# Loads of W of the in-projection issued by PoolE from the second quad on

## The chip, the core and the metric

The kernel runs on one core of one Trainium2 chip. The metric is the device time of one execution in microseconds (us); three executions of the kernel before are given. One further execution was taken by the hardware profiler, and all rows quoted below come from it. "Span" is the time from the program's first instruction to its last in that execution.

Engines are named as the profile names them: PE (TensorE matmul), PEld (its weight loads), DVE (VectorE), ACT (ScalarE), POOL (GpSimd, "PoolE" in the title) and SP (SyncE). SP does no arithmetic here; it only issues DMAs. SPq and POOLq in a row stand for the sequencer of that engine, which waits and issues.

## The reference

A decoder block with two mixing branches, cut to what matters here:

```
proj = x @ w_in[l] + b_in[l]          # x (2048, 1024), w_in (1024, 9216)
q, k, v, g_attn, u_lru, g_lru, gate_logits = split(proj)
attn  = three groups of causal dilated attention over rope(q), rope(k), v
y_a   = (attn * silu(g_attn)) @ w_attn_proj
h     = rg_lru(causal_conv(u_lru))
y_b   = (h * silu(g_lru)) @ w_lru_proj
merged = sigmoid(gA) * y_a + sigmoid(gB) * y_b
x     = layer_norm(alpha * x + merged @ w_out + b_out)
```

All is float32. The first line, the in-projection, is the largest part, and the change touches it alone.

## The kernel before

The program has three stages one after the other: the in-projection (with rope, the convolution, the recurrence and the gates folded in) up to about 1442 us of the span, the attention up to about 1640 us, and the output part.

**Quads.** The in-projection is cut into 72 quads, `s` = 0 to 71. A quad computes two tiles of 128 output columns for two chunks of 512 positions; quads 0 to 35 go over all 72 column tiles with the first two chunks, quads 36 to 71 over the same tiles with the last two. Over the 1024 inputs a quad is a 2 by 2 block product, done in seven block products in the manner of Strassen and Winograd instead of eight (quads 0 and 36 are plain, eight). One block product is a *job*: 12 matmuls of 128x128 by 128x512, four slices of the inputs by three terms (high by high, high by low, low by high part of a float32 value).

**What a quad needs of W.** Four blocks of W, A11, A12, A21 and A22, 128 partitions by 512 elements (256 KB) each, and four sums of them: S1 = A21 + A22, S2 = S1 + A11, S3 = A21 + A11, S4 = S2 + A12. ACT copies each of the seven into a high part `h`, DVE subtracts to get the low part `l` (`prep_w`), and PE multiplies with both. In the first 36 quads S1 and S3 start as two loads of A21, into which POOL adds A22 and A11 by an accumulating DMA (`added`, line 245); the low parts are stored to `wl_scr`. In the last 36 quads DVE forms the sums, POOL forms S4, and the low parts are loaded back from `wl_scr` (`load_lo`, line 287).

**Order.** Nothing is scheduled by a tool: the code walks over the jobs T, and each engine's instructions stand in the order in which this walk emits them. Each engine works through its own list strictly in order, and an instruction that waits for a semaphore holds all that stand behind it on that engine. `at(t, fn)` puts a piece of work at a job. With t0 three or four jobs ahead of a quad's first job, a quad of the first half loads S1 and S3 six jobs ahead of t0, A11 four, A12 three, A22 mostly a job before t0 or later, and adds into S1 and S3 four jobs ahead; DVE's first sum stands one job ahead of t0. In the second half A21 and A22 are loaded four jobs and A11 and A12 three jobs ahead of t0.

**Slots.** All these tiles, and also x, q, k, v and the recurrence's temporaries, live in 34 slots of 256 KB that are handed out in the order in which they were given back (`take`, `give`). A load has to wait until the slot's last reader, an engine or a store, is done.

**Who issues.** Before the change SP issues almost all DMAs: the loads of W (line 234), of x (221), the partition swaps for rope (`sw`, 307), the stores of low parts (282), of q, k and v (330, 337, 347, 371), of the recurrence's input (`u_scr`, 377) and others. POOL issues the accumulating DMAs, 64 small loads for the recurrence's gates (441) and four of a bias (445, 446), and does some arithmetic, mostly in the second half of the quads (S4, half of rope, the gating of the recurrence's output).

**The start.** The code first emits, on SP: A11 of quad 0, four blocks of x, A12, four blocks of x, A21 and A22, then eight blocks of x; only then come the five loads of quad 1. PE begins when the first W block and the first x block are there and split.

Of the kernel before, what the change touches and what calls it, by code (L numbers as in the profile page):

```python
# [15 lines left out]
P = 128  # L16
S = 2048
# [14 lines left out]
def hybrid_block_kernel(ctx: ExitStack, tc: tile.TileContext, a: dict, out: bass.AP):  # L32
    nc = tc.nc
    sp, act, dve, pool, pe = nc.sync, nc.scalar, nc.vector, nc.gpsimd, nc.tensor
# [98 lines left out]
    def take(name, dt=F32R):  # L133
        if not vacant:
            raise RuntimeError(f"no slot at {now['n']}: {[x[1].name if hasattr(x[1],'name') else x[1] for x in home.values()]} chains {len(chains)}")
        i = vacant[0]
        if name[0] == "y" and now["n"] >= base[NQ - 1]:
            i = next((x for x in LATE if x in vacant), i)
            if i in LATE:
                LATE.remove(i)  # L140
        vacant.remove(i)
        t = sl_p.tile([P, CH], dt, tag=f"s{i}", name=name)
        home[id(t)] = (i, t)
        return t
# [86 lines left out]

    def load_w(s, n):
        r = raw[s, n] = take(f"w{n}_{s}", F32)
        sp.dma_start(r.rearrange("p (k f) -> p k f", f=P), w_part(s, "A21" if n[0] == "S" else n))

    def w_part(s, n):

        f = plan[s][1][int(n[1]) - 1][0]
        k = 4 * (int(n[2]) - 1)
        return a["w_in"][f, :, k:k + 4, :]  # L240
# [461 lines left out]
    for s in range(1, NQ):  # L702
        t0 = base[s] - (3 if plan[s][0] else 4)
        if plan[s][2] is None:
            for d, n in ((4, "A21"), (4, "A11"), (3, "A22"), (3, "A12")):
                at(t0 - d, lambda s=s, n=n: load_w(s, n))
            for j in range(4):
                at(t0 + j, lambda s=s, j=j: prep_w(s, j))
            continue
        if plan[s][0]:  # L710
            for d, n in ((4, "A21"), (4, "A22"), (3, "A11"), (3, "A12")):
                at(t0 - d, lambda s=s, n=n: load_w(s, n))
        else:
            d22 = 3 if s == 1 else 4 - plan[s][2].index(4)
            for d, n in ((6, "S1"), (6, "S3"), (4, "A11"), (3, "A12"), (d22, "A22")):
                at(t0 - d, lambda s=s, n=n: load_w(s, n))
            for n, x in (("S1", "A22"), ("S3", "A11")):
                at(max(t0 - 4, 2), lambda s=s, n=n, x=x: added(s, n, x))
        at(max(t0 - 1, 4), lambda s=s: sums(s))
        at(max(t0, 4), lambda s=s: add_w(s, "S4", "S2", "A12"))  # L720
        if plan[s][0]:
            at(t0, lambda s=s: sum3(s))
        for j in range(7):
            d = 3 if j == 6 and plan[s][2] is MID else 0
            if plan[s][0] and j % 2 == 0:
                at(t0 + j - 1 + d, lambda s=s, j=j: load_lo(s, j))
            at(t0 + j + d, lambda s=s, j=j: prep_w(s, j))
# [244 lines left out]
    n = len(where)  # L972
# [416 lines left out]
    for n in range(32):  # L1389
        c, f = divmod(n, 8)  # L1390
# [229 lines left out]
```

## Time and profile before

| what | us |
|---|---|
| median of three executions | 2099.08 |
| lowest and highest of them | 2097.64 and 2104.75 |
| the profiled execution, own time | 2101.99 |
| its span | 2100.3 |
| SP's loads of W (wA 253, wS 70): median from issue to landing | 5.0 and 4.6 |

The page of the profile gives busy time by engine (its first part), the span in 40 slices (second), DMA queues (third), and groups of instructions. For single places the waits (who waited for whom), the timeline (instructions in order of time) and the table of stretches are read. In a timeline row the first number is the start, the second the duration in us, and a bracket at its end is the time the engine had been idle and what ended that. In the table of stretches the row gives the length, the busy time and the number of instructions of PE, PEld, DVE, ACT and POOL, then the granted clock of TensorE, the busy share of the 16 DMA engines and GB/s.

### The profile page before, as it was taken

The page shows a single profiled execution, that of the slowest core. Times are in us where ns is not written, and L with a number is a line of the kernel's source. Part 1 is how long each engine was busy: PE and PEld are TensorE (multiplying, and loading weights), DVE is VectorE, ACT ScalarE, POOL GpSimd, SP SyncE. Part 2 cuts the span into 40 slices and gives each one's busy share as a digit, 9 for nine tenths or more (in the row PEclk, how much of TensorE's full clock was granted, in tenths as well). Part 3 has the DMA queues.
Part 4 walks back from the last instruction along what each step waited for, and adds up shares of the span by engine and source line. Part 5 has one row for each costly group of instructions (what it writes and reads, how often), then busy time and mean ns, then how long its engine had stood idle before and what let it go on. Part 6 is the DMA issues. An engine that isn't in the chain of part 4 may idle for free. (4 is left out here: it accounts for less than half of the span.)

```text
span 2100.3 us, 35032 instructions
## 1 busy us (share of the span) xinstructions
PE 2070.4 (99%) x11696; PEld 1706.2 (81%) x11696; DVE 1676.0 (80%) x3146; ACT 1093.1 (52%) x2293; POOL 474.9 (23%) x436
## 2 busy tenths in 40 slices
PE   8999999999999999999999999999999999999998
PEld 7888788788778888888888887888888888888887
DVE  8889789788788778888879887976999645576667
ACT  6347356346256566657666565666999411211100
POOL 1111111111111012231222232221424344331120
PEclk9999999999999999999999999999999999999999
DMA  9898988998988977878788879789896798864431
GB/s 273 270 251 250 263 261 248 281 247 264 235 284 233 319 229 203 243 206 232 235 271 255 283 225 260 230 244 352 317 345 206 228 305 273 299 223 157 156 106 71
DMA packets 369589, 516.26 MB, mean 246 GB/s; under 512 B 173056, under 2 KB 178176, under 8 KB 366080
## 3 DMA queue, kind: packets, MB, share of 16 engines
q1 hardware_dynamic: 349232, 480.63, 71.6%
q0 software_dynamic: 12256, 19.42, 5.6%
q10 hardware_dynamic: 7920, 13.97, 1.9%
q8 instruction: 93, 1.52, 0.3%
q14 instruction: 88, 0.72, 0.1%
HBM read 312.95 MB, written 186.25 MB: 238 GB/s over the span
## 5 line engine op out<-in xcount | busy, mean ns | idle before, releaser
L632 PE MATMUL q<-xT,hS 128*128 128x512 f32 x1680 | 519.2, 390 | 0.5 <-DVE y L227 0.5
L632 PE MATMUL q<-xT,l 128*128 128x512 f32 x1120 | 436.2, 389 | 0.0
L632 PE MATMUL q<-xB,hA 128*128 128x512 f32 x1248 | 389.9, 394 | 5.8 <-ACT xB L215 5.8
L632 PEld LDWEIGHTS q<-xT,hS 128*128 128x128 f32 x1680 | 314.2, 188 | 70.8 <-issue 6.1
L632 PE MATMUL q<-xB,l 128*128 128x512 f32 x904 | 354.0, 392 | 5.8 <-DMA l<-wl_scr 3.5
L632 PEld LDWEIGHTS q<-xB,hA 128*128 128x128 f32 x1248 | 235.7, 190 | 59.3 <-ACT xB L215 5.7
L632 PEld LDWEIGHTS q<-xT,l 128*128 128x128 f32 x1120 | 210.6, 188 | 43.9
L632 PEld LDWEIGHTS q<-xB,l 128*128 128x128 f32 x904 | 170.8, 189 | 44.2 <-DMA l<-wl_scr 5.1
L269 ACT ACTIVATE hA<-wA 128x512 fp32r<-128x512 f32 x218 | 135.0, 622 | 86.8 <-DMA wA<-in_w_in_dram 54.5
L632 PE MATMUL q<-xT,hA 128*128 128x512 f32 x560 | 174.1, 392 | 0.0
L245 POOL DMA_DIRECT2D wS<-in_w_in_dram x70 | 62.0, 978 | 493.8 <-DMA wS<-in_w_in_dram 201.5
L1051 ACT ACTIVATE p<-p,sta 128x256 f32<-128x256 f32 (+1 forms) x384 | 172.7, 468 | 1.1 <-DVE sta L1043 1.1
L632 PE MATMUL q<-xB,hS 128*128 128x512 f32 x560 | 172.6, 389 | 0.0
L269 ACT ACTIVATE hS<-S 128x512 fp32r<-128x512 f32 x175 | 107.8, 623 | 88.9 <-DVE S L227 42.6
L227 POOL TENSOR_TENSOR S<-S,wA 128x512 f32<-128x512 f32 x35 | 50.1, 1431 | 415.6 <-DVE S L227 214.6
L632 PEld LDWEIGHTS q<-xT,hA 128*128 128x128 f32 x560 | 105.1, 189 | 24.0 <-issue 2.5
L632 PEld LDWEIGHTS q<-xB,hS 128*128 128x128 f32 x560 | 105.1, 188 | 22.1 <-issue 0.4
L227 DVE TENSOR_TENSOR y<-y,cos 128x512 f32<-128x512 f32 x96 | 85.0, 888 | 43.3 <-DMA sw<-y 38.3
L1043 DVE CUSTOM_DVE_ANT_0 p<-s,mask 128x256 f32<-128x256 f32 (+1 forms) x384 | 116.4, 360 | 0.2 <-PE s L1036 0.2
L1479 PE MATMUL z<-wo,mh 128*128 128x512 f32 (+1 forms) x264 | 101.0, 383 | 0.0
L1480 PE MATMUL z<-wo,ml 128*128 128x512 f32 (+1 forms) x264 | 101.0, 383 | 0.0
L1478 PE MATMUL z<-wo,mh 128*128 128x512 f32 (+1 forms) x264 | 101.0, 383 | 0.0
(204 smaller groups left out, 4163.6 us busy)
## 6 DMA issues: line engine op xcount, KB each, us to landing
wA<-in_w_in_dram SPq DMA_DIRECT2D x253, 256.0 KB, 5.0
wl_scr<-l SPq DMA_DIRECT2D x105, 512.0 KB, 5.3
l<-wl_scr SPq DMA_DIRECT2D x105, 512.0 KB, 4.6
sw<-y SPq DMA_DIRECT2D x384, 64.0 KB, 3.1
wS<-in_w_in_dram SPq DMA_DIRECT2D x70, 256.0 KB, 4.6
wS<-in_w_in_dram POOLq DMA_DIRECT2D x70, 256.0 KB, 6.5
v_scr<-vs SPq DMA_DIRECT2D x192, 64.0 KB, 3.9
B<-k_scr SPq DMA_DIRECT2D x24, 512.0 KB, 7.5
```

The source lines that it names most:

```text
L227: eng.tensor_tensor(out=out, in0=in0, in1=in1, op=op)
L245: pool.dma_start(t, w_part(s, x), accum_op=ALU.add)
L269: act.activation(h, r, AF.Copy)
L632: pe.matmul(bank, w[:, ks], x[:, kk, xx], start=(first and i == 0 and not onto), stop=(last and i == 11), skip_group_check=onto)
L1043: dve.tensor_tensor_reduce(out=st["p", i, j][:, h, lo:256], in0=st["s", i, j // 2][h][:, j % 2, lo:256], in1=mask[:, lo:256], scale=1.0, s ...
L1051: act.activation(p, p, AF.Exp, scale=-1.0, bias=s[:, h:h + 1], accum_out=s[:, 2 + h:3 + h])
L1478: pe.matmul(z, mh[:, k], w[:, 0, hs], start=(k == 0), stop=False)
L1479: pe.matmul(z, mh[:, k], w[:, 1, hs], start=False, stop=False)
L1480: pe.matmul(z, ml[:, k], w[:, 0, hs], start=False, stop=(k == 7))
```

## The change

In `load_w` the engine that issues is chosen by the quad: SP for quad 0, POOL for all others. That moves 319 DMAs of 256 KB: 175 in quads 1 to 35 (five each) and 144 in quads 36 to 71 (four each). The transfers, their sizes, their slots and the walk that emits them are the same; each load now stands in POOL's list, at the place where the walk emits it, instead of in SP's.

```
     def load_w(s, n):
         r = raw[s, n] = take(f"w{n}_{s}", F32)
-        sp.dma_start(r.rearrange("p (k f) -> p k f", f=P), w_part(s, "A21" if n[0] == "S" else n))
+        eng = pool if s else sp
+        eng.dma_start(r.rearrange("p (k f) -> p k f", f=P), w_part(s, "A21" if n[0] == "S" else n))
```

One line is added, so every line number from 235 on is larger by one afterwards: the loads of W on POOL are line 235, the accumulating DMAs line 246.

How the lists change at three places. Names are tile, then quad, then a running number: `wA12_29` is A12 of quad 29.

The start of POOL's list before, from the last instruction that builds the mask on; then come the accumulating DMAs of quad 1:

```order
L70 AFFINE_SELECT mask_185<-mask_185 128x128
L245 DMA wS1_1_311<-in_w_in_dram 128x512
L245 DMA wS3_1_313<-in_w_in_dram 128x512
L445 DMA brh_200<-in_lru_vec_dram 64x8
L446 DMA brh_200<-in_lru_vec_dram 64x8
```

The same place now; L235 are the loads of quads 1 and 2, L246 the accumulating DMAs:

```order
L70 AFFINE_SELECT mask_185<-mask_185 128x128
L235 DMA wS1_1_311<-in_w_in_dram 128x512
L235 DMA wS3_1_313<-in_w_in_dram 128x512
L235 DMA wA11_1_315<-in_w_in_dram 128x512
L235 DMA wA12_1_345<-in_w_in_dram 128x512
L235 DMA wA22_1_347<-in_w_in_dram 128x512
L246 DMA wS1_1_311<-in_w_in_dram 128x512
L246 DMA wS3_1_313<-in_w_in_dram 128x512
L235 DMA wS1_2_444<-in_w_in_dram 128x512
```

The five loads of quad 1 stood behind all loads of x on SP; now nothing but the mask stands ahead of them, and the two accumulating DMAs follow at once.

SP's list before, around the loads of quad 29 (some 565 to 575 us of the span); `u_scr6` is the store of a recurrence input, `v_scr20` are stores of v:

```order
L234 DMA wA22_28_5627<-in_w_in_dram 128x512
L234 DMA wS1_29_5632<-in_w_in_dram 128x512
L234 DMA wS3_29_5634<-in_w_in_dram 128x512
L371 DMA v_scr20_79<-vs32_1_5434 32x16x32
L337 DMA qh_scr11_114<-rp11_0_5604 2048x1x32
L377 DMA u_scr6_175<-y46_1_5637 128x512
L371 DMA v_scr20_79<-vs32_1_5434 32x16x32
L234 DMA wA11_29_5685<-in_w_in_dram 128x512
L282 DMA wl_scr28_145<-l0_28_5601 128x1024
L371 DMA v_scr20_79<-vs32_1_5434 32x16x32
L234 DMA wA12_29_5714<-in_w_in_dram 128x512
```

POOL's list now, around the same loads; `gr0` are the small loads for the gates:

```order
L235 DMA wA12_28_5517<-in_w_in_dram 128x512
L442 DMA gr0_201<-in_wr_dram 64x64
L442 DMA gr0_201<-in_wi_dram 64x64 x2
L442 DMA gr0_201<-in_wr_dram 64x64
L235 DMA wA22_28_5627<-in_w_in_dram 128x512
L235 DMA wS1_29_5632<-in_w_in_dram 128x512
L235 DMA wS3_29_5634<-in_w_in_dram 128x512
L235 DMA wA11_29_5685<-in_w_in_dram 128x512
L246 DMA wS1_29_5632<-in_w_in_dram 128x512
L246 DMA wS3_29_5634<-in_w_in_dram 128x512
L235 DMA wA12_29_5714<-in_w_in_dram 128x512
```

On SP, A11 and A12 of quad 29 stood behind the stores of q, u and v, each of which waits for DVE; on POOL they stand behind other loads of W and behind the accumulating DMAs, which wait for the loads of S1 and S3 to land.

## The prediction

> **What bounds the kernel now.** First the page: the span, two engines, and the DMA engines' share by fortieths of it.
>
> ```profile
> span 2100.3 us, 35032 instructions
> PE 2070.4 (99%) x11696; PEld 1706.2 (81%) x11696; DVE 1676.0 (80%) x3146; ACT 1093.1 (52%) x2293; POOL 474.9 (23%) x436
> DMA  9898988998988977878788879789896798864431
> ```
>
> PE is idle for 29.9 us of 2100.3. No change of the loads can give more than the part of this that hangs on loads, with what the idle time itself costs. SP issues the last load of wA at 1404.7 us (the row of the tile wA below), so the attention and the output part only move with what comes before. POOL has room; the DMA engines have little in the first half.
>
> Next, what PE waited for. These rows stand in the waits of PE for the whole span (total us, times, longest); those left out are attention.
>
> ```profile
> PE q L632 <- ACT xB L215: 5.8, 1, 5.8
> PE g L493 <- DVE vl L227: 5.1, 2, 2.6
> PE q L632 <- DMA l<-wl_scr: 3.5, 3, 2.0
> PE q L632 <- DVE l L227: 2.2, 2, 1.2
> PE g L493 <- ACT vh L483: 2.0, 1, 2.0
> ...
> PE q L632 <- DVE y L227: 0.5, 1, 0.5
> ```
>
> The first is the start, where nothing can be multiplied yet. The other five come to 13.3 us: that is what lies on PE in the in-projection. Two of them, `vl` and `vh`, I followed back to W, in the timelines of PE, DVE, ACT, SP and POOL around quad 29 and around the same event in quad 13 (the first row):
>
> ```profile
> 261.86 0.50 PE L493 MATMUL g<-vl,gw 64*128 64x512 f32 x2 [2.64 <-DVE vl L227]
> 259.91 0.69 DVE L227 TENSOR_TENSOR S<-S,wA 128x512 f32<-128x512 f32 x1 [1.93 <-DMA wA<-in_w_in_dram]
> ...
> 566.91 3.02 SPq L377 DMA_DIRECT2D u_scr<-y  x1
> 569.98 1.61 SPq L371 DMA_DIRECT2D v_scr<-vs  x1
> 571.64 0.67 SPq L234 DMA_DIRECT2D wA<-in_w_in_dram  x1
> ...
> 573.31 1.26 SPq L234 DMA_DIRECT2D wA<-in_w_in_dram  x1
> ...
> 569.73 1.81 POOL L245 DMA_DIRECT2D wS<-in_w_in_dram  x2 [26.47 <-DVE ub L575]
> 577.73 0.63 ACT L269 ACTIVATE hA<-wA 128x512 fp32r<-128x512 f32 x1 [5.13 <-DMA wA<-in_w_in_dram]
> 577.72 0.69 DVE L227 TENSOR_TENSOR S<-wS,wA 128x512 f32<-128x512 f32 x1 [2.60 <-DMA wA<-in_w_in_dram]
> 578.93 0.51 PE L493 MATMUL g<-vh,gw 64*128 64x512 f32 x2 [2.00 <-ACT vh L483]
> 581.91 0.79 PE L493 MATMUL g<-vl,gw 64*128 64x512 f32 x2 [2.48 <-DVE vl L227]
> ```
>
> SP stood 4.6 us on two stores (566.91 and 569.98), and only then issued A11 and A12 of quad 29. ACT and DVE then waited 5.13 and 2.60 us for them, and behind those waits on the same engines stood `vh` and `vl`, for which PE waited 2.00 and 2.48. The idle PE costs more than its idle time, as the granted clock (third column from the end) in the table of stretches shows; the rows that begin at 50 and 720 us are for comparison:
>
> ```profile
> 50.00:400.00 350.00, 347.36 (x1539) 284.14 (x1537) 296.12 (x485) 176.10 (x290) 48.37 (x60) 1.00 0.90 262
> 581.00:589.00 8.00, 7.09 (x20) 5.20 (x21) 6.95 (x12) 5.49 (x10) 1.75 (x2) 0.57 1.01 367
> 720.00:1250.00 530.00, 530.00 (x2355) 430.93 (x2354) 443.73 (x590) 339.38 (x549) 130.04 (x104) 1.00 0.80 241
> 1301.00:1305.00 4.00, 4.00 (x14) 2.48 (x13) 1.60 (x3) 2.38 (x4) 0.00 (x0) 0.57 1.15 408
> ```
>
> After the gaps at 579 to 582 the clock is 0.57 for 8.0 us, 3.4 us lost; after the last wait for `l<-wl_scr` it is 0.57 for 4.0 us, 1.7 us lost. So 13.3 + 5.1 = 18.4 us is the most that can be won. The rows also give a job: 530 us / 2355 = 0.225 us a matmul, 2.7 us a job, 18.9 us a quad of seven.
>
> **Part by part.** *319 issues leave SP and go to POOL.* Prices, from the page, the tiles wA and wS (least, median and most ns of one issue) and the waits of POOL:
>
> ```profile
> L234 SPq DMA_DIRECT2D wA<-in_w_in_dram x253: 327/438/3436, 0.8 to 1404.7; - x127
> ...
> wA<-in_w_in_dram SPq DMA_DIRECT2D x253, 256.0 KB, 5.0
> wS<-in_w_in_dram POOLq DMA_DIRECT2D x70, 256.0 KB, 6.5
> ...
> L245 POOL DMA_DIRECT2D wS<-in_w_in_dram x70: 853/909/1244, 19.3 to 686.7; - x70
> ...
> q1 hardware_dynamic: 349232, 480.63, 71.6%
> q0 software_dynamic: 12256, 19.42, 5.6%
> POOL wS L245 <- DMA wS<-in_w_in_dram: 201.5, 16, 23.9
> ```
>
> POOL pays about 0.91 us each, 319 x 0.91 = 290 us. Per quad of 18.9 us that is five loads or 4.5 us in the first half, on a POOL that is busy 48.37 of 350 us (14%, then 38%), and four or 3.6 us in the second (130.04 of 530, 25%, then 44%). POOL is not filled. Landing may take 6.5 instead of 5.0 us, though that row is of accumulating DMAs; 1.5 us is the upper price, nothing the lower, and I take 1.
>
> *Are the loads issued earlier or later?* The last row: POOL stood 201.5 us in 16 waits at accumulating DMAs because SP had not yet brought the tile. POOL is ahead of SP, by up to 23.9 us, in the first half. At quad 29 its last work before 569.73 had been 26.47 us earlier, so A11 could go when its slot came free, not when u and v had been stored. In the second half arithmetic stands between the loads on POOL, and I expect little either way. So the loads come some us earlier where SP was stuck, and 1 us later elsewhere.
>
> *Waits on W, quads 13 and 29:* 2.64 + 2.00 + 2.48 = 7.1 us, and 3.4 us of clock. Between nothing and 10.5 I take all 10.5: when SP got to these loads POOL had had nothing to do for 26.47 us (quad 29, row 569.73) and 23.9 us (quad 13, the longest wait in the last row), and the waits to be covered are 5.13 us at most.
>
> *Other waits of PE:* `l` from DVE and `y` (2.7 us) lie behind rope swaps that SP issues, and `l<-wl_scr` (3.5, and 1.7 of clock) behind SP's list at 1277 to 1300 us. SP loses the W issues between them, but still waits for DVE there. Bounds 0 and 7.9; half, 3.9.
>
> *The start.* Here the change costs. Timelines of the first 22 us, and two stretches:
>
> ```profile
> 4.00:8.00 4.00, 2.25 (x5) 1.52 (x6) 2.73 (x4) 2.93 (x5) 0.00 (x0) 1.00 1.04 360
> ...
> 12.00:16.00 4.00, 4.00 (x19) 3.19 (x18) 3.97 (x13) 3.14 (x6) 0.00 (x0) 1.00 1.05 399
> 1.82 0.29 POOL L70 TENSOR_SCALAR_AFFINE_SELECT mask<-mask 128x128 f32<-128x128 f32 x1
> 19.28 2.00 POOL L245 DMA_DIRECT2D wS<-in_w_in_dram  x2 [17.16 <-DMA wS<-in_w_in_dram]
> ...
> 7.59 5.62 SPq L221 DMA_DIRECT2D xcB<-in_xT_dram  x8
> 10.22 1.98 ACT L215 ACTIVATE xB<-xcB 128x512 fp32r<-128x512 f32 x3 [0.57 <-DMA xcB<-in_xT_dram]
> 10.88 2.05 DVE L216 TENSOR_TENSOR xB<-xcB,xB 128x512 fp32r<-128x512 f32 x3 [0.51 <-ACT xB L215]
> 11.32 0.63 PE L632 MATMUL q<-xB,hA 128*128 128x512 f32 x2
> ```
>
> The DMA engines are full (1.04, 1.05), and x is used as it comes: ACT waits 0.57 us for the second slice of PE's second job, DVE finishes its low part at 10.88 + 2.05 / 3 = 11.56, and the job, begun at 11.32, wants it three matmuls later, at 12.0. The slack is 0.4 us. POOL is free from 2.1 us on, so quad 1's five loads and two accumulating DMAs now go in among x and W of quad 0 instead of behind them. A load takes 262144 B / 399 GB/s = 0.66 us of the full engines. An accumulating one costs 1.9 of that: 5.6% / 19.42 MB = 0.288 against 71.6% / 480.63 = 0.149. Together 5 x 0.66 + 2 x 1.27 = 5.8 us of delay for x, less 0.4 us of slack: **5.4 us**. Bounds: 0, as PE shows no wait there now, and 7.1, when the next two loads (1.3 us) get in as well. The Trainium skill, DMA: Bandwidth & Descriptors, section "Issuing engines are not separate DMA queues", speaks against the change here: DMAs of all issuers run on the same 16 engines and interleave, and another issuer saves only issue time. By that rule the 5.4 us stand and little else is won.
>
> *New waits.* Later landings elsewhere, POOL's arithmetic behind loads that wait for a slot: between 0 and 6 us, of which I take 2. Less than nothing is excluded here, since what SP gains is counted above.
>
> **Sum**, against the profiled execution's own 2101.99 us: +5.4 - 10.5 - 3.9 + 2 = -7.0, so 2095.0. That execution lay 2.9 us above the median 2099.08, so on the median: 2092.1, **2092 us**.
>
> **Rivals.** (a) *The start costs nothing*, because SP's transfers keep their rate: then -12.4, 2087 us. For it: later jobs have more slack than the second. Against it: the share of 1.04. (b) *No gain:* the waits of ACT and DVE go, but others take their place, since DVE is busy 85% (296.12 of 350) and DMA 90%; half of the 14.4 us won (7.2), less 2 new and 5.4 at the start: 0, 2099 us. W was then hidden anyhow. (c) *Slower, by DMA time.* If plain packets of POOL's queue cost what its accumulating ones do, 0.288 instead of 0.149% a MB, then the first half's 175 loads, 45.9 MB, need 45.9 x 0.00139 x 2100.3 = 134 us more of the engines. At a share of 0.90 only 72 us of the first 720 are free: +62, 2161 us. It decides from 0.222% a MB on. Against it: an accumulation reads its destination too, a plain load doesn't. (d) *Slower, by issue:* the start costs 7.1 and new waits 2, nothing is won, because POOL's issues are held up. A11 is loaded three jobs, 8.1 us, ahead of its sum; with 6.5 us to land, 1.6 us are left. An issue that is held for longer than this makes DVE wait in each quad, and beyond DVE's idle 15% (2.8 us a quad) PE too: 2099 + 9.1 = 2108 us. The rows speak against it: the slowest of 70 issues took 0.39 us more than the fastest, beside a DVE busy for 85%. The Trainium skill, SBUF — State Buffer, section "SBUF: two separate sides", has a rule to this effect: while VectorE runs an instruction that takes both ports, GpSimd cannot write descriptors. No row here shows a stall of that size.
>
> **Chances.** Forecast 0.42 (2087 to 2097), (a) 0.20, (b) 0.21, (c) 0.07, (d) 0.10. About 0.3%, 6.3 us, is what a measurement can tell from no change: faster means under 2092.8, slower over 2105.4. Of the forecast's case 0.26 lies below 2092.8 and 0.16 above; with (a) 0.46 faster, with (b) 0.37 same, (c) and (d) 0.17 slower. The range goes from 2083 (all 18.4 won, 2 back) to 2106, and leaves out (c), most of (d) and the tails. The forecast's own range is 2087 to 2097.
>
> **What would show it.** Right: no waits of ACT and DVE for wA near 256 and 577 us, no wait of PE at 262 and 579 to 582, a granted clock of 1.00 there; but x late and PE waiting in the first 25 us, its first attention matmul earlier by some 7 us. Wrong: no wait of PE at the start (a); new waits of PE for `l`, `vl` or `vh` elsewhere in the first 720 us (b); a DMA share near 1.0 from 50 to 720 us (c); issues of POOL over 2.5 us and waits for wA in every quad (d).

## The result, and the profile after

The changed kernel takes **2118.07 us** (median of 4 runs, 2116.04 to 2120.69), the kernel before 2098.55 us beside it (4 runs). The ratio is 1.0087, with an interval of 1.0065 to 1.0110: **slower by 0.87%**, 19.5 us. The forecast was 2092 us, the range 2083 to 2106. The profiled execution of the change took 2117.2 us (span 2115.5), that of before 2101.99 (2100.3), so the two traces differ by 15.2 us. The first of them lies 0.9 us under its median and the second 3.4 us over the 2098.55; with the 15.2 that makes up the 19.5.

The page of the changed kernel, at the places shown of before:

```profile
span 2115.5 us, 35183 instructions
PE 2075.4 (98%) x11696; PEld 1707.5 (81%) x11696; DVE 1692.5 (80%) x3146; ACT 1093.9 (52%) x2293; POOL 645.2 (30%) x755
DMA  7986978998887977778788879879896798964431
q1 hardware_dynamic: 303296, 396.99, 58.7%
q0 software_dynamic: 37776, 103.06, 18.0%
```

The two queues answer rival (c) at once. POOL's queue moved 103.06 MB instead of 19.42 in 18.0% instead of 5.6% of the engines' time: 12.4% for 83.6 MB, 0.148% a MB, and SP's queue pays 58.7 / 396.99 = 0.148 on the mean of all that it moves. Both queues together took 77.2% of 2100.3 us before and 76.7% of 2115.5 now, 1621 and 1623 us. So a plain load costs the engines the same from either issuer. POOL's issues are cheap too: 0.54 to 0.56 us in the middle, 1.32 at most (lines L235 of the tiles wS and wA), where the sum had 0.91 and rival (d) needed 2.5.

```profile
L235 POOL DMA_DIRECT2D wS<-in_w_in_dram x70: 538/538/750, 2.1 to 700.2; - x70
L235 POOL DMA_DIRECT2D wA<-in_w_in_dram x249: 538/556/1317, 3.3 to 1416.4; - x125
```

What PE waited for in the whole span (total us, times, longest):

```profile
PE q L633 <- DVE y L227: 14.1, 4, 7.3
PE q L633 <- ACT xB L215: 7.2, 3, 5.7
PE q L633 <- DVE l L227: 1.4, 2, 1.1
PE q L633 <- ACT hA L270: 1.2, 1, 1.2
PE g L494 <- ACT ti L506: 1.1, 2, 0.9
...
PE g L494 <- DVE vl L227: 0.6, 2, 0.3
...
PE g L494 <- ACT vh L484: 0.2, 1, 0.2
```

The waits that were to go are gone: `vl` fell from 5.1 to 0.6, `vh` from 2.0 to 0.2, and `l<-wl_scr` from 3.5 to nothing. One that was 0.5 us is now 14.1: `y`, in four pieces. The start (`xB`) grew from 5.8 to 7.2.

Idle time is not the whole price, as the clock drops behind a gap. So the table of stretches is read by the number of matmuls that fit into a stretch (third column, in brackets, behind PE), at the 0.225 us of one that the prediction found. First the kernel before, then the change:

```profile
0.00:25.00 25.00, 19.17 (x71) 14.75 (x72) 18.50 (x36) 16.27 (x26) 5.59 (x15) 1.00 0.94 308
25.00:720.00 695.00, 685.20 (x3017) 559.12 (x3016) 590.59 (x941) 359.60 (x594) 92.51 (x112) 1.00 0.89 260
...
1250.00:1340.00 90.00, 86.47 (x376) 68.76 (x375) 73.82 (x93) 57.75 (x89) 27.35 (x21) 0.98 0.81 239
```

```profile
0.00:25.00 25.00, 16.50 (x39) 9.40 (x40) 11.69 (x26) 12.45 (x20) 9.30 (x22) 1.00 0.92 307
25.00:720.00 695.00, 677.66 (x2969) 551.53 (x2968) 587.82 (x931) 351.60 (x581) 186.46 (x280) 0.99 0.86 252
720.00:1250.00 530.00, 530.00 (x2356) 431.14 (x2355) 450.22 (x591) 345.60 (x557) 180.67 (x210) 1.00 0.81 244
1250.00:1340.00 90.00, 90.00 (x402) 72.96 (x401) 78.66 (x99) 59.09 (x96) 32.87 (x39) 1.00 0.87 258
```

- **Start:** 32 matmuls fewer in 25 us, 7.2 us lost.
- **25 to 720 us:** 48 fewer, 10.8 us lost. The DMA engines are no fuller (0.86 instead of 0.89).
- **720 to 1250 us:** no difference.
- **1250 to 1340 us:** 26 more, 5.9 us won; the waits for `l<-wl_scr` and their clock.
- **Behind PE's last matmul:** the span ends 11.0 us after it instead of 7.4. 3.6 us lost.

Together 7.2 + 10.8 - 5.9 + 3.6 = 15.7, for the 15.2 us between the traces.

**The start.** The timelines of POOL and SP in the change, then two stretches:

```profile
2.07 1.30 POOL L235 DMA_DIRECT2D wS<-in_w_in_dram  x2
3.35 1.60 POOL L235 DMA_DIRECT2D wA<-in_w_in_dram  x3
8.77 1.84 POOL L246 DMA_DIRECT2D wS<-in_w_in_dram  x2 [3.81 <-DMA wS<-in_w_in_dram]
...
10.60 9.67 SPq L221 DMA_DIRECT2D xcB<-in_xT_dram  x8
```

```profile
8.00:12.00 4.00, 3.31 (x7) 1.31 (x5) 1.39 (x2) 1.26 (x2) 1.80 (x2) 1.00 1.02 383
12.00:16.00 4.00, 3.26 (x7) 1.90 (x7) 2.09 (x4) 2.52 (x4) 0.57 (x1) 1.00 1.08 287
```

POOL's five loads and two accumulating DMAs go out from 2.07 us on; SP's last eight blocks of x take 9.67 us to issue, from 10.60, where before they took 5.62 from 7.59. From 12 to 16 us PE does 7 matmuls instead of 19, at 0.47 us each: it not only waits, it also runs slowly between the waits. In the trace of before a matmul starts 0.43 us or more after the one ahead of it until 11.3 us, and in the change until 18.3 us; soon behind these times it is 0.23. (The trace's records of the clock begin at just these two times, so the 1.00 of the rows ahead of them rests on no record.) PE's idle time in the first 25 us grew by 2.7 us; the rest of the 7.2 is this longer slow stretch.

**The first half.** One event, in quad 13, is 7.29 of the 14.1 us. The rows are from the timelines of POOL, SP, DVE and PE:

```profile
251.85 0.54 POOL L235 DMA_DIRECT2D wA<-in_w_in_dram  x1 [4.13 <-DVE rp L227]
252.38 1.89 POOL L246 DMA_DIRECT2D wS<-in_w_in_dram  x2
...
254.32 4.96 SPq L308 DMA_DIRECT2D sw<-y  x4
...
263.82 0.69 DVE L227 TENSOR_TENSOR y<-y,cos 128x512 f32<-128x512 f32 x1 [8.40 <-DMA sw<-y]
...
265.86 1.19 PE L633 MATMUL q<-xT,hS 128*128 128x512 f32 x2 [7.29 <-DVE y L227]
```

```profile
248.00:252.00 4.00, 4.00 (x19) 3.21 (x18) 4.00 (x8) 0.54 (x2) 0.15 (x1) 1.00 1.03 297
252.00:256.00 4.00, 4.00 (x19) 3.30 (x19) 2.62 (x5) 1.99 (x5) 2.21 (x3) 1.00 1.06 225
...
260.60:270.80 10.20, 4.94 (x12) 3.91 (x13) 5.73 (x9) 4.93 (x9) 1.10 (x2) 0.50 0.95 248
588.00:595.00 7.00, 4.65 (x11) 3.71 (x12) 5.45 (x9) 4.64 (x9) 1.09 (x2) 0.52 0.93 260
```

A rope chain swaps the rows of `y` by four DMAs of SP into `sw`; DVE then multiplies. Just ahead of such a swap POOL put a load and two accumulating DMAs on DMA engines that were full (1.03, 1.06). The issue of its four DMAs took 4.96 us and DVE stood 8.40 us for it; behind that wait on DVE stood the `y` that frees PE's bank. The same swap before, the two accumulating DMAs that went out 9 us behind it, and the DMA share around it:

```profile
240.99 3.00 SPq L307 DMA_DIRECT2D sw<-y  x4
249.82 1.82 POOL L245 DMA_DIRECT2D wS<-in_w_in_dram  x2 [23.93 <-DMA wS<-in_w_in_dram]
240.00:244.00 4.00, 4.00 (x19) 3.30 (x19) 3.21 (x6) 2.40 (x5) 0.00 (x0) 1.00 0.86 261
244.00:248.00 4.00, 4.00 (x20) 3.30 (x19) 2.62 (x6) 0.52 (x1) 0.00 (x0) 1.00 0.73 176
```

There DVE stood 1.38 us for it. In the change the store of k ahead of the swap also held SP longer (4.36 us instead of 2.06), so not all of the delay is the swap's own transfer. From 260.6 us on the clock was 0.50 for 10.2 us. Half of that lies in the wait itself; in the other half PE was busy for 4.94 us with 12 matmuls, for which 2.7 us are enough, so the clock cost another 2.2 us. The same happened at 590 us: 5.61 us of waiting, then 4.65 us for 11 matmuls, which lost 2.2 us more. Over the stretch from 25 to 720 us the swaps land later (median us, from the DMA issues), and DVE's wait for them grew; first before, then the change:

```profile
sw<-y SPq DMA_DIRECT2D x192, 64.0 KB, 3.0
DVE y L227 <- DMA sw<-y: 35.9, 19, 3.7
```

```profile
sw<-y SPq DMA_DIRECT2D x192, 64.0 KB, 4.1
DVE y L227 <- DMA sw<-y: 59.1, 22, 8.4
```

### The profile page after: what moved, and what is told of

It is laid out like the page before. It is cut to its first block, busy times and chain, and to the rows that moved or that the text cites. A ratio compares the mean times of both kernels' runs of the same rounds, so it can differ in the third digit from the quotient of the medians.

```text
span 2115.5 us, 35183 instructions
## 1 busy us (share of the span) xinstructions
PE 2075.4 (98%) x11696; PEld 1707.5 (81%) x11696; DVE 1692.5 (80%) x3146; ACT 1093.9 (52%) x2293; POOL 645.2 (30%) x755
## 3 DMA queue, kind: packets, MB, share of 16 engines
q1 hardware_dynamic: 303296, 396.99, 58.7%
q0 software_dynamic: 37776, 103.06, 18.0%
## 4 chain that ended last, share of the span: by engine, by line
PE 65%; ACT 6%; DMA 1%; DVE 0%; SPq 0%; issue 0%; DVEq 0%; ACTq 0%
PE q L633 40%; ACT p L1052 6%; PE yb L1369 3%; PE yb L1370 3%; PE z L1480 3%; PE z L1479 3%; PE yb L1371 3%; PE z L1481 3%; PE ya L1448 1%; PE ya L1447 1%; PE ya L1449 1%; PE o L1093 1%; PE g L494 1%; ACT ptb L1076 1%; PE pt L1063 1%; PE s L1037 1%
## 5 line engine op out<-in xcount | busy, mean ns | idle before, releaser
L633 PE MATMUL q<-xT,hS 128*128 128x512 f32 x1680 | 522.9, 393 | 14.1 <-DVE y L227 14.1
L235 POOL DMA_DIRECT2D wA<-in_w_in_dram x249 | 146.3, 589 | 489.1 <-DVE l L227 132.3
L1453 POOL TENSOR_TENSOR me<-gA,ybr 128x512 f32<-128x512 f32 x32 | 49.8, 1567 | 180.6 <-DVE gA L1452 180.6
L1480 PE MATMUL z<-wo,mh 128*128 128x512 f32 (+1 forms) x264 | 101.0, 383 | 0.0
```

The lines of the kernel that those rows point to most:

```text
L235: eng.dma_start(r.rearrange("p (k f) -> p k f", f=P), w_part(s, "A21" if n[0] == "S" else n))
L633: pe.matmul(bank, w[:, ks], x[:, kk, xx], start=(first and i == 0 and not onto), stop=(last and i == 11), skip_group_check=onto)
L1480: pe.matmul(z, mh[:, k], w[:, 1, hs], start=False, stop=False)
```

## The experiments

Three questions were put in turn: where the loss lies (e1 to e4, and e7 for the start), what makes a swap late (e5, e6, e8 to e10, e12), and what the end costs (e11, e13 to e15). In the table each ratio is against runs of the kernel before on the same chip; "25 to 720" is the number of matmuls in that stretch against the 3017 of before, at 0.225 us each; the next two columns are totals in the same stretch. These three are of one execution each. Programs that are the same up to the loads of quad 36, near 700 us, show what that is worth: e3, e11, e13 and e15 have 3037, 3028, 3033 and 3036 matmuls in the stretch, so a difference under some 2 us says nothing.

| run | median us | ratio, interval | 25 to 720, us | DVE waits for sw | PE waits for y |
|---|---|---|---|---|---|
| before | 2098.6 | 1 | 0 | 35.9 | 0.5 |
| the change | 2118.1 | 1.0087, 1.0065 to 1.0110 | +10.8 | 59.1 | 14.1 |
| e1 | 2113.4 | 1.0064, 1.0042 to 1.0085 | +15.1 | 64.6 | 17.0 |
| e2 | 2098.7 | 0.9990, 0.9981 to 1.0000 | +0.9 | 36.7 | 0.6 |
| e3 | 2093.2 | 0.9970, 0.9957 to 0.9982 | -4.5 | 40.8 | 2.5 |
| e4 | 2106.1 | 1.0029, 1.0017 to 1.0041 | +4.7 | 57.0 | 9.4 |
| e5 | 2096.5 | 0.9984, 0.9973 to 0.9996 | -6.8 | 44.8 | 3.1 |
| e6 | 2084.4 | 0.9927, 0.9910 to 0.9945 | -11.7 | 30.3 | 0 |
| e7 | 2096.0 | 0.9980, 0.9969 to 0.9992 | -4.7 | 42.9 | 0.7 |
| e8 | 2131.7 | 1.0149, 1.0124 to 1.0174 | +26.1 | 38.4 | 0 |
| e9 | 2096.8 | 0.9974, 0.9965 to 0.9984 | +1.1 | 50.3 | 8.2 |
| e10 | 2106.7 | 1.0031, 1.0020 to 1.0041 | +4.1 | 53.5 | 2.0 |
| e12 | 2115.9 | 1.0070, 1.0053 to 1.0087 | +16.0 | 1.2 | 0 |

**e1: the start undone.**

```
-        eng = pool if s else sp
+        eng = pool if s > 2 else sp
```

> As the change, but the loads of quads 1 and 2 stay on SP; from quad 3 on they are POOL's. Theory T1 (three separate things: x crowded out at the start, waits for y near 265 and 590 us, a gain near 1300 us): the start's 7.1 us go and the rest stays, 2118 - 7 = 2111 us. Rival T2 (the waits near 265 and 590 us only come from the shift that the late start gave to the engines' order in time): they go too, 2118 - 19 = 2099 us or less. Rival T3 (the start is no part of it, since what is late there is caught up): 2118 us.

Between T1 and T3: 4.6 us less. In the first 25 us there are 71 matmuls again, as before, so the 7.2 us of the start are its own and are given back in full; but the stretch to 720 us then loses 15.1 us instead of 10.8. T2 falls: the waits for `y` don't come from the late start, they are there without it, and larger (17.0 us).

**e2: the second half alone.**

```
-        eng = pool if s else sp
+        eng = pool if plan[s][0] else sp
```

> Only the loads of quads 36 to 71 are POOL's, those of the first half are SP's as before. Theory T1: only the gain near 1300 us is left, 2098.5 - 6 = 2092.6 us. Rival T4 (that gain is a by-product of the late first half, and POOL's issues cost something in the second half too): 2098.5 to 2102 us.

As T4 has it, no change to speak of. But the gain is there: the stretch from 1250 to 1340 us is as full as in the change (401 matmuls), and PE's last matmul ends 5.0 us earlier than before. The span gained only 2.6 of them. What eats the rest is behind PE's end, below.

**e3 and e4: the loads of wA alone, and those of wS alone, in the first half.**

```
-        eng = pool if s else sp
+        eng = pool if s > 2 and (plan[s][0] or n[0] != "S") else sp     (e3)
+        eng = pool if s > 2 and (plan[s][0] or n[0] == "S") else sp     (e4)
```

> From quad 3 on; in the first half POOL takes the three loads of wA alone, and SP keeps the two of wS, behind which the accumulating DMAs wait. In the second half all four are POOL's. Theory T1a (the swaps are late because the accumulating DMAs, of 1.9 times the DMA time, come earlier and in bunches): these stay where they were, so 2092.6 to 2096 us. Rival T1b (any load that POOL issues ahead of SP's list takes the DMA engines from the swaps): three of five loads, 2111 less two fifths of the 11 us, about 2104 to 2107 us.

> The complement: from quad 3 on, in the first half POOL takes the two loads of wS with their accumulating DMAs, and SP keeps the three of wA. In the second half all four are POOL's. Theory T1a (accumulations come earlier): all of the loss of the first half but that of the start, 2110 us. Rival T1b (any load): two fifths of 11 us, 2097 to 2100 us.

e3 beats both kernels: 2093.2 us, 0.30% under before. e4 loses 7.4 us against e2. Of PE's waits between 25 and 720 us these are the largest, e3 above, e4 below:

```profile
PE g L494 <- DVE vl L227: 3.1, 3, 1.6
PE q L633 <- DVE y L227: 2.5, 2, 1.8
PE q L633 <- DVE l L227: 1.4, 2, 1.2
```

```profile
PE q L633 <- DVE y L227: 9.4, 2, 5.3
PE q L633 <- DVE l L227: 2.0, 1, 2.0
```

e3 lies in T1a's range; e4 lies between the two ranges. It looked like T1a, the accumulating DMAs. But the two parts don't add up: e2 - 5.5 (wA) + 7.4 (wS) is 2100.6 us, and e1, which moves both, took 2113.4.

**e5 and e6: the same as e4 and e2, with the accumulating DMAs made plain.**

```
-        pool.dma_start(t, w_part(s, x), accum_op=ALU.add)
+        pool.dma_start(t, w_part(s, x))
```

> As e4 (wS and its accumulating DMAs on POOL early, 2106.1 us), but the second load onto each wS overwrites instead of accumulating, so that the sums S1 and S3 are left out. Theory T1a (the swaps are late because the accumulating DMAs take 1.9 times the DMA time of a load): the 7.4 us between e4 and e2 shrink to what e6 does not also gain, e5 - e6 is 0 to 2 us. Rival T1b (they are late because anything that POOL issues gets ahead of SP's list, whatever it costs): e5 - e6 stays 5 to 8 us.

> The control: as e2 (2098.7 us), the sums S1 and S3 left out in the same way; SP brings wS and wA of the first half. Under both theories only the waits for W near 262 and 580 us shrink, some 3 to 7 us: 2092 to 2096 us.

T1a falls: e5 - e6 is 12.1 us, not 0 to 2. Part of the 12.1 lies at the end of the program, where POOL's closing DRAIN (see below) took 10.33 us in e5 and 4.61 in e6; PE's last matmul ends 6.7 us later in e5 than in e6, and 4.3 us later in e4 than in e2. Less DMA time is worth much in both (9.6 and 14.3 us for 70 DMAs; the control came out well under its range), so the engines' time is short. But with the dearer DMAs out of the way, wS on POOL still costs as much or more. It is its coming early that costs, not the kind of DMA.

**e7: wA from quad 1 on.**

```
-        eng = pool if s > 2 and (plan[s][0] or n[0] != "S") else sp
+        eng = pool if s and (plan[s][0] or n[0] != "S") else sp
```

> As e3 (wA alone on POOL in the first half, 2093.2 us), but from quad 1 on instead of quad 3. If x is crowded out at the start by any early load: three of quad 1 at 0.66 us each and up to three of quad 2, 2 to 4 us more than e3, 2095 to 2097 us. If the accumulating DMAs do it: nothing, 2093 us.

2096.0 us, 2.9 more than e3, though the two intervals overlap. The first 25 us are clearer: 62 matmuls, 9 fewer than before, 2.0 us. So three early plain loads crowd x out as well, and the start's 7.2 us are not for the accumulating two alone.

**e8: POOL held to SP's place.**

```
+        if n == "S1" and 2 < s and not plan[s][0]:
+            sp.dma_start(tok[0:1, s % 6:s % 6 + 1], a["b_in"][0:1, 0:1])
+            pool.tensor_copy(tok2[0:1, s % 6:s % 6 + 1], tok[0:1, s % 6:s % 6 + 1])
         eng = pool if s > 2 and (plan[s][0] or n[0] == "S") else sp
```

> As e4, but ahead of the loads of wS of each quad POOL waits for a DMA of 4 bytes that SP issues where it issued these loads before, so that POOL cannot get ahead of SP's list. Theory T-order (the loss of e4 is that wS and its accumulations overtake the swaps in SP's list): it goes, 2098 to 2101 us, as e2, and the waits of PE for y near 255 and 577 us are under 2 us. Rival T-pool (the loss is in POOL's queue itself, slower or held up by DVE): it stays, 2106 us or more.

The time missed both theories: 2131.7 us. The waits did not. PE has no wait for `y` over 0.1 us any more, and DVE's wait for the swaps fell from 57.0 to 38.4 us, near the 35.9 of before. But the 4-byte DMA has to land before POOL may go on, so W is now late, and DVE waits for wS. DVE's waits between 25 and 720 us in e8:

```profile
DVE y L229 <- DMA sw<-y: 38.4, 20, 6.1
DVE S L229 <- DMA wS<-in_w_in_dram: 35.3, 11, 6.4
```

So the swaps behave as T-order has it, and a token of this kind is no cure. It is no clean proof: with W late, a swap may have more room in any case.

**e9: one load of five left with SP.**

```
-        eng = pool if s else sp
+        eng = pool if s > 2 and (plan[s][0] or n != "S3") else sp
```

> From quad 3 on all loads on POOL but one: in the first half SP keeps S3, the second of wS. POOL's accumulating DMA onto S3 then waits for SP once in each quad, and everything behind it on POOL waits too. Theory T-pace (e3 is fast because these waits hold POOL back to the pace of SP's list, so that its loads cannot get ahead of the swaps): near e3, 2093 to 2099 us. Rival T-share (the loss grows with the part of W that POOL brings): four of five loads of the first half, between e3 with three (2093.2) and e1 with five (2113.4), 2103 to 2107 us.

2096.8 us, as T-pace has it: 16.6 us less than e1 for one load in five, 3.0 of them by a shorter closing DRAIN of POOL (see below). POOL's accumulating DMA onto S3 waits for SP, and all that stands behind it on POOL waits with it. PE still waits 8.2 us for `y`, against 17.0 in e1 and 2.5 in e3, so this cures less than e3 does. POOL's waits between 25 and 720 us, in the change, then e3, then e9:

```profile
POOL wS L246 <- DMA wS<-in_w_in_dram: 33.1, 19, 3.7
```

```profile
POOL wS L246 <- DMA wS<-in_w_in_dram: 66.6, 11, 9.7
```

```profile
POOL wS L246 <- DMA wS<-in_w_in_dram: 68.4, 16, 8.1
```

The size of this wait isn't the measure: e4 has 100.1 us of it, for loads that POOL itself had issued, and e7 has 42.6. What the wait does shows in when a DMA goes out, in us from the start of the job at which the code emits it (mean over quads 3 to 35):

| run | S1 | S3 | A11 | adding into S1, S3 | A12 | A22 |
|---|---|---|---|---|---|---|
| before | 4.3 | 5.0 | 4.6 | 4.5, 5.4 | 5.2 | 3.7 |
| the change | -0.3 | 1.2 | 0.8 | 2.1, 3.1 | 2.0 | -1.6 |
| e3 | 4.3 | 5.0 | 0.9 | 5.5, 6.2 | 4.4 | -1.7 |
| e4 | -2.1 | 0.6 | 4.4 | -1.3, 0.9 | 5.4 | 4.0 |
| e9 | -0.5 | 4.0 | 0.6 | 2.1, 5.5 | 3.8 | -2.0 |

T-pace is right for what stands behind an accumulating DMA, A12 above all, but not for A11 and A22: these go out as early in e3 as in the change, and do no harm there. What the slow runs have early and e3 has not are S1, S3 and the DMAs that add into them. Why these and not A11 and A22 isn't shown. That A12 too is held back in e3 may be why wA and wS don't add up.

**e10: as e1, but wS of quads 11 to 15 and 27 to 31 stays with SP.**

```
-        eng = pool if s else sp
+        eng = pool if s > 2 and not (n[0] == "S" and (11 <= s < 16 or 27 <= s < 32)) else sp
```

> As e1 (2113.4 us), but in quads 11 to 15 and 27 to 31 SP keeps the loads of wS, as in e3. Theory T-local (the loss is made in the two stretches near 240 to 265 and 575 to 590 us, where the DMA engines are full and a swap has no room): nearly all of the 20.3 us between e1 and e3 goes, 2093 to 2099 us. Rival T-all (W is early everywhere, and the loss is made all over the first half, and shows up there only): 10 of 33 quads, 2105 to 2109 us.

2106.7 us, by T-all. PE's wait for `y` falls from 17.0 to 2.0 us as the two stretches are relieved, but 6.3 us of waits for `l`, in four pieces, come in elsewhere. Ten quads of 33 give back 6.7 of 20.3 us. The profiled execution, at 2103.3 us, was the fastest of the eight; in it the stretch gained more, 11.0 of the 19.6 us between e1 and e3. So the two big events are not the whole loss, but how large their part is stays open.

**e12: the swaps issued by ACT.**

```
-            sp.dma_start(flat(sw)[32 * b:32 * b + 32], flat(rw)[32 * (b ^ 1):32 * (b ^ 1) + 32])
+            (act if c < 2 else sp).dma_start(flat(sw)[32 * b:32 * b + 32], flat(rw)[32 * (b ^ 1):32 * (b ^ 1) + 32])
```

> As e1 (2113.4 us), but the four swaps of each rope chain of the first half are issued by ACT instead of SP, so that they don't stand behind SP's stores. Theory T-engines (a swap is late because its transfer shares the DMA engines with W that was issued ahead of it): who issues it changes nothing, its landing stays near 4.2 us, PE still waits for y, 2108 to 2118 us. Rival T-SP (it is late because SP holds it back, for instance behind the store to k_scr that waits 4 us for DVE): the waits for y go, 2094 to 2104 us. Above 2118 us ACT itself holds the swaps up, behind its own waits, and nothing is told apart.

The landing stayed as T-engines has it, at 4.2 us from a queue of ACT's own, and so did the time, 2115.9. But the waits for `y` went, as T-SP has it, and others came: ACT stands at the swap until DVE has made `y`, and DVE then waits for ACT's high parts. The swaps' landing in e12, and DVE's waits there between 25 and 720 us (in e1 `hA` and `hS` were 16.6 and 13.8):

```profile
sw<-y ACTq DMA_DIRECT2D x192, 64.0 KB, 4.2
```

```profile
DVE l L227 <- ACT hA L270: 63.7, 36, 4.8
DVE l L227 <- ACT hS L270: 39.3, 30, 4.6
...
DVE y L227 <- DMA sw<-y: 1.2, 1, 1.2
```

That a swap lands late whoever issues it is shown. The median landing alone doesn't make a kernel slow, though: from 25 to 720 us it is 3.8 us in e3 and 3.7 in e4. How much of DVE's wait is transfer and how much SP's holding back isn't shown, as ACT's own waits cover it.

**The end: e11, e13, e14, e15.** All engines meet at the end of the program, and there the trace's records (the views leave them out) hold a DRAIN on POOL behind its last instruction. It took 4.40 us before, and ended 0.7 us before SP's own last DRAIN; in the change it took 8.65 us and ended 3.6 us behind it. Four edits moved loads back to SP:

```
+        eng = pool if 2 < s < 36 and n[0] != "S" else sp                          (e11)
+        eng = pool if 2 < s < 66 and (plan[s][0] or n[0] != "S") else sp          (e13)
+        eng = pool if 0 < s < 60 else sp                                         (e14)
+        eng = pool if s >= 42 or 2 < s < 36 and n[0] != "S" else sp               (e15)
```

> Only wA of quads 3 to 35 on POOL; in the second half all loads are SP's again. If e3 is the sum of two parts (first half -5.5 us, second half -0.9 us against 2099.6): 2094 us. If the second half's part is larger than e2 showed, because PE's own end came 5.0 us earlier there: 2097 to 2099 us.

> As e3 (2093.2 us), but the last 24 loads, of quads 66 to 71, are SP's. Theory T-ring (the DRAIN with which POOL ends takes 4.4 to 10.3 us by how many DMAs POOL issued: plotted against the number of extra loads it rises by some 0.09 us a load and falls back every 53 or so, and two pairs of kernels with the same DMAs agreed to 4 ns): 219 extra loads instead of 243 put it near its low point, 4.4 to 5.5 us instead of 6.77, and the time is 1 to 2 us less, 2091 to 2092 us. Rival T-end (the DRAIN follows what runs at the end): it stays 6.8 us, 2093 us.

> As the change (2118.1 us), but the last 48 loads, of quads 60 to 71, are SP's: 271 extra loads on POOL instead of 319. Theory T-ring: POOL's closing DRAIN is 4.4 to 5 us instead of 8.65, and the time 3 to 4 us less, 2114 to 2115 us. Rival T-end: DRAIN near 8.6 us, 2118 us.

> As e3 (2093.2 us), but instead of the last 24 loads the first 24 of the second half, of quads 36 to 41, are SP's: 219 extra loads on POOL as in e13, and the loads beside the waits for l<-wl_scr stay with POOL. Theory T-ring: the DRAIN is 4.77 us as in e13 though what runs at the end differs, PE's last matmul ends as in e3 (2082 us, give or take 1), and the span is 1.5 to 2 us shorter than the 2091.5 of e3; the time 2091 to 2092 us. Rival T-end: the DRAIN is 6.8 us as in e3, 2093 us.

| run | loads moved | DRAIN us | PE's last end | span | median us | ratio, interval |
|---|---|---|---|---|---|---|
| before | 0 | 4.40 | 2092.9 | 2100.3 | 2098.6 | 1 |
| the change | 319 | 8.65 | 2104.5 | 2115.5 | 2118.1 | 1.0087, 1.0065 to 1.0110 |
| e2 | 144 | 7.51 | 2087.9 | 2097.7 | 2098.7 | 0.9990, 0.9981 to 1.0000 |
| e3 | 243 | 6.77 | 2082.4 | 2091.5 | 2093.2 | 0.9970, 0.9957 to 0.9982 |
| e11 | 99 | 8.61 | 2089.3 | 2100.3 | 2100.9 | 1.0002, 0.9990 to 1.0015 |
| e13 | 219 | 4.77 | 2085.0 | 2092.1 | 2093.0 | 0.9965, 0.9952 to 0.9978 |
| e14 | 271 | 4.73 | 2108.8 | 2116.1 | 2120.3 | 1.0095, 1.0076 to 1.0113 |
| e15 | 219 | 9.30 | 2083.4 | 2095.0 | 2095.4 | 0.9984, 0.9975 to 0.9993 |

In e11 both answers missed: PE ends 3.6 us earlier than before, the program just as late. e13 and e14 had the DRAIN where T-ring put it, 4.77 and 4.73 us; but PE's own end came 2.6 us after e3's and 4.3 after the change's. In e14 SP brought W again beside the loads of `l<-wl_scr`, and PE waited for those 3.4 us. In e13 only 1.1 us are lost there (395 matmuls instead of 400 from 1250 to 1340 us); 1.6 us are lost before 720 us, where its program is that of e3, and so by chance. e15 then moved the same number of loads as e13, and its DRAIN took 9.30. **T-ring falls:** the number alone doesn't set it, and "what runs at the end" doesn't either, as e3 and e15 end alike with 6.77 and 9.30. The DRAIN does set the time, though: e15's PE ends 1.7 us before e13's, and its span 2.9 us after. What sets it stays open.

## Why the prediction was wrong

The step that failed is **"New waits ... between 0 and 6 us, of which I take 2"**, and with it, under "Are the loads issued earlier or later?", the thought that a load which comes earlier can only help. From 25 to 720 us the sum had the waits of quads 13 and 29 go (-10.5). The waits did go, but the stretch came out 10.8 us longer, so what came in cost some 20 us: 14 of it idle time of PE for `y`, 4.4 slow matmuls behind the two longest of these waits; the rest is small pieces.

- **Start, +5.4:** the mechanism was right, the size not: 7.2 us, which e1 gives back in the same stretch. That the upper bound of 7.1 comes near is luck: it stands for two more loads, while what came on top of PE's waits were its slow matmuls (0.43 us each up to 18.3 us, and before only up to 11.3), which no term had.
- **Waits at quads 13 and 29, -10.5:** the waits went as said (`vl` and `vh` 7.1 to 0.8 us). The clock behind them did not: 0.50 and 0.52 at the same two places, behind the waits for `y`. The price of 3.4 us was also too high. Its row, 581 to 589 us, has 20 matmuls, 4.5 us of work, so 3.5 us are lost in it, and 0.9 of these are idle time that the 2.48 had counted already.
- **Half of the other waits, -3.9:** `l` stayed about where it was (2.2 to 1.4), `y` grew, and `l<-wl_scr` gave all of its 3.5 us and its clock (5.9 in all), not half.
- **Rival (b)** named what happened, waits taking the place of waits on full DMA engines, but priced it so that it ended at nothing. It took the DMA share as a mean; at 248 to 256 us the share was over 1.
- **Rivals (c) and (d)** were wrong in their mechanisms: 0.148% a MB, and no issue above 1.32 us.
- **The end, 3.6 us,** was in no term.
- **"POOL is ahead of SP, by up to 23.9 us"** misread the wait: POOL had no work between one quad's sums and the next. SP's loads went out 4.5 us behind the job that emits them, and this is about what POOL could win.

What the sum had missed is in the order of one list. SP worked in order, 4 to 5 us behind the place where the code puts a load; so W came late, but it came behind the swaps that stood ahead of it and SP's own waits on DVE kept it there. On POOL the loads only wait for a slot. In the change the 99 loads of wA in quads 3 to 35 were issued 0.4 us, on average, after the start of the job at which the code emits them, and 4.5 us before; the 66 of wS 0.5 and 4.7 us; the swaps stayed 6.9 us behind (6.5 before). So W overtook the swaps. For wA alone this did no harm: in e7 its loads went out 0.1 us after their job and the stretch gained 4.7 us. The harm comes with wS and the DMAs that add into it (e4), which is what e8 takes away, at a price, and e9 halves.

The prediction weighed the Trainium skill, DMA: Bandwidth & Descriptors, section "Issuing engines are not separate DMA queues", which says that all issuers' DMAs interleave on the same 16 engines and another issuer saves issue time alone. The swaps landed in 4.1 us beside POOL's loads, and in 4.2 from SP (e1) as from ACT (e12); the trace agrees, as far as the rule goes: it says nothing of who comes first. The same page, section "SWDGE vs HWDGE vs iDMA", says that inside an engine the queues of the two kinds are served in turn; by that a swap would share the engine with W that another issuer sent. No run here shows these inner queues.

## What to carry to other kernels

In this kernel the issuer's list, worked through in order, was also a priority: bulk loads that stood behind small, urgent transfers in it could not overtake them. Before such loads get an issuer of their own, look at what they will now be ahead of, and read the DMA share in slices of a few us where the urgent ones go, not as a mean. Moving part of them, so that the new issuer still waits for the old one now and then (e3, e9), kept a gain here: 2093 and 2097 us against 2099 and 2118.

## What the runs showed of the hardware

- POOL's closing DRAIN took between 4.40 and 10.33 us (e5) in these kernels, and in most of them it ended last, up to 5.6 us behind SP's own (e5). Kernels with the same list of POOL's DMAs agreed closely (e4 and e8: 8.607 and 8.604 us; e1 and e12: 7.912 and 7.910), but neither the number of DMAs nor what runs at the end gave the rule.
- Loads that moved from SP's queue to POOL's took the DMA engines the same time there, 0.148% of the span a MB, and POOL issued one in 0.54 to 0.56 us, where an accumulating one took 0.94 (medians).
- DVE was slightly slower beside POOL's loads: from 720 to 1250 us it did 590 instructions in 443.73 us before and 591 in 450.22 in the change, 1.3% more each. In e11, where POOL issues no loads of W in this stretch, it took 445.62 for 593, as before. PE lost nothing by it there.
